# Gate tables of a PEER layer: one-hots of four tokens laid out as two contiguous blocks of two tokens

## The chip, the core and the metric

One core of a Trainium2 chip runs the whole program as one launch. The metric is the device time of that launch in microseconds. Before the change it is 3511.7 us, the median of three runs (3500.95 to 3513.11).

The engines that matter here: PE (TensorE), which runs matmuls and loads their weights (PEld); DVE (VectorE); ACT (ScalarE); POOL (GpSimd); and the queues that start transfers. Each engine runs its own instructions in a fixed order and waits on semaphores for the others.

## What is computed

One layer of a decoder over 1056 tokens: a token mixer (RWKV7 and pooling), then PEER, a layer of 16384 single-neuron experts of which each token uses 8 x 16, then an embedding gate and a norm. The change lies in PEER. Cut to that:

```python
s1 = jnp.einsum('thc,nc->thn', q[:, :, 0], sub_keys[0]);  s2 = ...(q[:, :, 1], sub_keys[1])
v1, i1 = lax.top_k(s1, 16);  v2, i2 = lax.top_k(s2, 16)
cand = v1[..., :, None] + v2[..., None, :]                # 256 candidates per head
sc, ci = lax.top_k(cand, 16)
expert = e1 * 128 + e2                                     # e1, e2: the two keys chosen
gate = softmax(sc)
act = gelu(einsum('thkd,td->thk', u_tab[expert], xb)) * gate
out = einsum('thk,thkd->td', act, v_tab[expert])
```

## The kernel before

The 1056 tokens are split. The first 672 are "dense": for them the kernel multiplies with all 16384 experts and scales the result by a gate table, which is zero for experts that a token does not use. The other 384 tokens gather the rows of their experts.

The program has three stages. First come the mixer and its projections (to about 520 us). Then, for four groups of tokens, three streams are interleaved by hand (`merge`): the recurrent chunks, the projections of PEER (`phase_c`, with matmuls at lines 661 to 663 and 747), and the selection of experts (`top` and `select`, many short DVE instructions at 762 to 850), at whose end the gate tables of dense tokens are made. Last comes the dense phase (`ublock`, `ugate`, `vblock`, line 1075), in which PE multiplies with the expert tables while GpSimd fetches rows for the other tokens. The order of the instructions on each engine is fixed when the program is built, by a scheduler that follows the order of the program and its own estimates.

A gate table is made like this. For one token, the table over the 128 x 128 experts is a product of two one-hot matrices: the 128 choices of the token lie on the partitions, `e16[:, 0]` and `e16[:, 1]` hold the two keys of each choice, `e16[:, 2]` and `e16[:, 3]` the upper and lower part of its gate in f16. The loop at 871 does four tokens at a time, 168 times in all (672 / 4). The tile `ab` (three buffers, f16) holds three blocks for four tokens, and the four tokens are innermost: [128 partitions, 3, 128 keys, 4 tokens].

- Line 875 (DVE): both one-hots in one instruction of 1024 elements, the keys `iota16` compared with `e16[:, 0:2]`, into blocks 0 and 1.
- Line 877 (DVE): block 2 = block 1 times the upper part of the gate, 512 elements.
- Line 878 (`GLO`, defined at 1043): block 1 = block 1 times the lower part, 512 elements; on GpSimd (through `PTT`, line 124), but on DVE where t is a multiple of 12, 58 times.
- Line 881 (PE): eight f16 matmuls of 128 x 128 x 128; weights are blocks 2 and 1, the moving operand is block 0. Token i is read with `[:, k, :, i]`, every fourth element.
- Line 882 (ACT): PSUM, four tokens of 128 columns, to the staging tile `st`; after 32 tokens line 884 stores it.

`iota16` is written once, by an iota on GpSimd (1040) and a cast on DVE (1041).

Of the kernel before, what the change touches and what calls it, by code (L numbers as in the profile page):

```python
# [10 lines left out]
F32 = mybir.dt.float32  # L11
F32R = mybir.dt.float32r
F16 = mybir.dt.float16
# [3 lines left out]
ALU = mybir.AluOpType  # L17
# [29 lines left out]
TC = 32  # L47
NTC = ND // TC
EB = 128
# [12 lines left out]
def body(ctx, tc, io):  # L62
    nc = tc.nc
    mm = nc.tensor.matmul
    TT, STT, TS, ACT = (nc.vector.tensor_tensor, nc.vector.scalar_tensor_tensor, nc.vector.tensor_scalar,
                        nc.scalar.activation)
# [17 lines left out]
    def v3(ap, n):  # L84
        return ap.rearrange("p (a b) -> p a b", b=n)
# [5 lines left out]
    def vec(base, i):  # L91
# [13 lines left out]
                   allow_small_or_imprecise_dtypes=True)  # L105
# [20 lines left out]
    def PS(tag):  # L126
        return pools[tag].tile([128, 512], F32, name="ps", tag=tag)
# [625 lines left out]
    def top(tk, pos, m):  # L753
        V12 = tk.tile([128, HEADS, 2, TOPK], F32, name="V12", bufs=1)
        I12 = tk.tile([128, HEADS, 2, TOPK], U32, name="I12", bufs=1)
        for i in range(16):
            if i % 4 == 0:
                sq = tk.tile([128, 4, 128], F32, name="scq", bufs=2)
                nc.sync.dma_start(sq[:m], sc_d[TIDX[pos], :m, i:i + 4, :])
            s_ = sq[:m, i % 4, :]  # L760
            v8, i8 = V12[:m, i // 2, i % 2, :], I12[:m, i // 2, i % 2, :]
            nc.vector.max(v8[:, 0:8], s_)
            nc.vector.max_index(i8[:, 0:8], v8[:, 0:8], s_)
            s2 = tk.tile([128, 128], F32, name="s2", bufs=2)
            nc.vector.match_replace(s2[:m], v8[:, 0:8], s_, -BIG)
            nc.vector.max(v8[:, 8:16], s2[:m])
            nc.vector.max_index(i8[:, 8:16], v8[:, 8:16], s2[:m])
            yield
        yield from select(tk, pos, m, V12, I12)


    def select(tk, col, m, V12, I12):
# [6 lines left out]
        for src, dst, add in ((V12, cand, TT), (F12, code, PTT)):  # L779
            off = 0  # L780
            for a, b, w in SEG:
                k = b - a
# [77 lines left out]
        ps = PS("b3")  # L860
# [3 lines left out]
        e16 = gp.tile([128, 4, 128], F16, name="e16")  # L864
# [4 lines left out]
        for t1 in range(0, m, TC):  # L869
            st = gp.tile([128, EB, TC], F32, name="gst", bufs=2)  # L870
            for t2 in range(0, TC, 4):
                ps = PS("b3")
                t = t1 + t2
                ab = gp.tile([128, 3, EB, 4], F16, name="ab", bufs=3)
                TT(ab[:, 0:2], iota16[:, None, :, :].to_broadcast([128, 2, EB, 4]),  # L875
                   e16[:, 0:2, None, t:t + 4].to_broadcast([128, 2, EB, 4]), op=ALU.is_equal)
                TT(ab[:, 2], ab[:, 1], e16[:, 2, None, t:t + 4].to_broadcast([128, EB, 4]), op=ALU.mult)  # L877
                GLO(t)(ab[:, 1], ab[:, 1], e16[:, 3, None, t:t + 4].to_broadcast([128, EB, 4]), op=ALU.mult)
                for i in range(4):
                    for k in (2, 1):  # L880
                        mm(ps[:, i * 128:(i + 1) * 128], ab[:, k, :, i], ab[:, 0, :, i], start=k == 2, stop=k == 1)  # L881
                ACT(st[:, :, t2:t2 + 4].rearrange("p e t -> p t e"), v3(ps, 128), AF.Copy, scale=1.0 / GS)  # L882
                yield
            nc.sync.dma_start(g_d[:, :, (col + t1 - GA) // TC].rearrange("g p e t -> p g e t"), st.rearrange("p (g e) t -> p g e t", e=GQ))
# [150 lines left out]
    tk = phases.enter_context(tc.tile_pool(name="tk", bufs=1))  # L1035
    gstack = ExitStack()
    gp = gstack.enter_context(tc.tile_pool(name="gp", bufs=1))
    iota16 = gp.tile([128, EB, 4], F16, name="iota16")
    it = gp.tile([128, EB, TC], F32, name="gst", bufs=2)[:, :, 0:4]
    nc.gpsimd.iota(it, pattern=[[1, EB], [0, 4]], base=0, channel_multiplier=0, allow_small_or_imprecise_dtypes=True)  # L1040
    nc.vector.tensor_copy(iota16, it)

    def GLO(t):
        return PTT if t % 12 else TT
# [125 lines left out]
    for col in range(0, GT, 128):  # L1170
# [31 lines left out]
        for half in range(2):  # L1202
            ps = dpt.tile([128, 512], F32, name="pt")
# [151 lines left out]
def program(arrays, extra=()):  # L1355
    nc = bacc.Bacc("TRN2", target_bir_lowering=False, num_devices=1)
    io = {k: nc.dram_tensor(k, v.shape, mybir.dt.from_np(v.dtype), kind="ExternalInput").ap()
          for k, v in arrays.items()}
    for k, s in list(OUTS.items()) + list(extra):
        io[k] = nc.dram_tensor(k, s, F32, kind="ExternalOutput").ap()  # L1360
    with tile.TileContext(nc, schedule_with_timeline_sim=True) as tc, ExitStack() as ctx:
        body(ctx, tc, io)
    return nc
# [15 lines left out]
```

## Time and profile before

| what | value |
|---|---|
| median of three runs | 3511.7 us |
| the profiled execution's own time | 3494.25 us |
| its span, first to last instruction | 3492.4 us |
| PE busy | 3262.7 us (93%) |
| DVE busy | 2675.0 us (77%) |
| POOL busy | 1769.3 us (51%) |
| ACT busy | 1179.8 us (34%) |
| first one-hot (line 875) to last start of an eviction (line 882) | 771.8 to 1370.6 us |

How to read it: all of it comes from one profiled execution, traced by the hardware. A busy time is the time during which an engine has at least one instruction running. Matmuls and DVE instructions are pipelined, so the shown time of one can overlap that of the next; what one costs in a row of its kind is the distance from start to start. [...] A share over the whole span is a mean over stages that have different limits.

### The profile page before, as it was taken

Reading aid. Unit: us, or ns where it says so; the run is one execution under the profiler, and the core shown is the slowest. Engines: PE = TensorE matmul, PEld = TensorE weight load, DVE = VectorE, ACT = ScalarE, POOL = GpSimd, SP = SyncE. Lnnn points to the kernel's source line nnn. Section 1 sums busy time; section 2 is a strip of 40 time slices with the busy share of each in tenths; the row PEclk is TensorE's granted clock in tenths of the full one; section 3 lists DMA queues with packets and bytes.
Section 4 is the critical chain, followed back from the end, with each engine's and each line's share of the span. In section 5 each row is a group of like instructions: output and inputs, shape, how many; then the busy total and the mean of one; then the engine's idle time right before and its main releaser. Section 6 shows DMA issues by size and latency. Waiting matters only on the chain.

```text
span 3492.4 us, 57600 instructions
## 1 busy us (share of the span) xinstructions
PE 3262.7 (93%) x21831; PEld 3150.6 (90%) x21831; DVE 2675.0 (77%) x5366; ACT 1179.8 (34%) x1776; POOL 1769.3 (51%) x1433
## 2 busy tenths in 40 slices
PE   8997998999999899999999999999999999999997
PEld 7876998989989788999999999999999999999997
DVE  6767333279999799978788778878888787788866
ACT  6452424345556455322122122122122212222243
POOL 5434234145465454156656555555555565555635
PEclk9998999999999899999999999999999999999999
DMA  5667645767767867479888888889898898898834
GB/s 177 213 197 177 185 134 148 213 174 231 210 194 212 282 199 258 131 278 318 308 315 307 306 320 311 313 318 317 314 321 315 307 312 308 301 318 313 311 123 132
DMA packets 467861, 883.61 MB, mean 253 GB/s; under 512 B 129280, under 2 KB 252416, under 8 KB 463104
## 3 DMA queue, kind: packets, MB, share of 16 engines
q1 hardware_dynamic: 356992, 477.24, 43.5%
q0 software_dynamic: 110592, 402.70, 32.6%
q8 instruction: 171, 2.80, 0.3%
q14 instruction: 106, 0.87, 0.1%
HBM read 759.22 MB, written 120.60 MB: 252 GB/s over the span
## 4 chain that ended last, share of the span: by engine, by line
DMA 26%; PE 22%; DVE 19%; issue 14%; POOL 11%; ACT 1%; SPq 0%; POOLq 0%; DVEq 0%; ACTq 0%
DMA row<-v,idx 14%; POOL row L1179 10%; DMA row<-u,idx 7%; PE pd L1075 7%; PE ps L881 2%; DVE ab L875 2%; PE ps L663 2%; PE ps L661 2%; DVE row L1187 2%; PE ps L662 2%; DVE elo L1063 1%; DVE po L1196 1%; PE ps L526 1%; DVE ab L877 1%; DMA sraw<-wq 1%
## 5 line engine op out<-in xcount | busy, mean ns | idle before, releaser
L1179 POOL DMA_INDIRECT row<-u,idx x384 | 534.9, 1393 | 387.9 <-DVE row L1187 248.4
L1179 POOL DMA_INDIRECT row<-v,idx x384 | 520.5, 1355 | 377.3 <-DVE po L1196 222.4
L1196 DVE SCALAR_TENSOR_TENSOR po<-row,act,po 128x1024 f32<-128x1024 f32 x381 | 488.8, 1283 | 152.6 <-DMA row<-v,idx 147.8
L1187 DVE SCALAR_TENSOR_TENSOR row<-row,xt 128x1024 f32<-128x1024 f32 x384 | 463.6, 1222 | 179.4 <-DMA row<-u,idx 177.8
L1075 PE MATMUL pd<-XH,elo 128*128 128x336 f32 x2176 | 524.9, 323 | 52.2 <-DVE elo L1063 49.3
L1061 ACT ACTIVATE ehi<-eraw 128x1024 fp32r<-128x1024 f32 x278 | 293.0, 1054 | 750.3 <-PE pd L1075 676.1
L1075 PE MATMUL pd<-wh,elo 128*128 128x336 f32 (+1 forms) x2112 | 509.5, 320 | 31.2 <-DVE elo L1063 30.9
L1075 PE MATMUL pd<-XH,ehi 128*128 128x336 f32 x2176 | 518.0, 319 | 4.1 <-DVE OT L1150 2.3
L1075 PE MATMUL pd<-XL,ehi 128*128 128x336 f32 x2176 | 519.5, 320 | 0.0
L1075 PE MATMUL pd<-wh,ehi 128*128 128x336 f32 (+1 forms) x2112 | 506.5, 319 | 8.7 <-DVE tg L1260 6.3
L1075 PE MATMUL pd<-wl,ehi 128*128 128x336 f32 (+1 forms) x2112 | 504.3, 318 | 0.0
L1075 PEld LDWEIGHTS pd<-XH,elo 128*128 128x128 f32 x2176 | 376.9, 191 | 64.4 <-DVE elo L1063 61.5
L1075 PEld LDWEIGHTS pd<-wh,elo 128*128 128x128 f32 x2112 | 362.1, 189 | 40.1 <-DVE elo L1063 39.4
L1075 PEld LDWEIGHTS pd<-XH,ehi 128*128 128x128 f32 x2176 | 377.7, 192 | 5.1 <-ACT wt L1081 2.5
L1075 PEld LDWEIGHTS pd<-XL,ehi 128*128 128x128 f32 x2176 | 376.7, 191 | 0.2
L1075 PEld LDWEIGHTS pd<-wh,ehi 128*128 128x128 f32 x2112 | 364.2, 189 | 10.5 <-issue 8.4
L1075 PEld LDWEIGHTS pd<-wl,ehi 128*128 128x128 f32 x2112 | 364.3, 189 | 0.0
L1063 DVE TENSOR_TENSOR elo<-eraw,ehi 128x1024 fp32r<-128x1024 f32 x257 | 317.9, 1237 | 11.7 <-ACT ehi L1061 6.3
L1140 ACT ACTIVATE wh<-wt 128x672 fp32r<-128x672 f32 x128 | 97.5, 766 | 662.1 <-DVE wt L1138 662.1
L881 PE MATMUL ps<-ab 128*128 128x128 f16 x1344 | 195.9, 295 | 25.0 <-DVE ab L877 12.0
L124 POOL TENSOR_TENSOR ab<-ab,e 128x512 f16<-128x512 f16 x110 | 128.4, 1169 | 172.2 <-DVE ab L877 130.7
L882 ACT ACTIVATE gst<-ps 128x512 f32<-128x512 f32 x168 | 179.5, 1103 | 94.4 <-PE ps L881 92.5
(499 smaller groups left out, 5962.7 us busy)
## 6 DMA issues: line engine op xcount, KB each, us to landing
eraw<-uT SPq DMA_DIRECT2D x128, 512.0 KB, 5.4
eraw<-vP SPq DMA_DIRECT2D x128, 512.0 KB, 5.7
g_d<-gst SPq DMA_DIRECT2D x21, 2048.0 KB, 8.4
gq<-g_d SPq DMA_DIRECT2D x32, 1344.0 KB, 9.4
whi<-wc_d SPq DMA_DIRECT2D x148, 256.0 KB, 4.4
wlo<-wc_d SPq DMA_DIRECT2D x148, 256.0 KB, 4.7
wc_d<-shi SPq DMA_DIRECT2D x40, 256.0 KB, 2.6
wc_d<-slo SPq DMA_DIRECT2D x40, 256.0 KB, 3.1
```

The source lines that it names most:

```text
L124: nc.gpsimd.tensor_tensor(out, a, b, op=op)
L661: mm(ps[:, :n], whi[:, kk, :], xhi[:, k, :n], start=k == 0, stop=False)
L662: mm(ps[:, :n], whi[:, kk, :], xlo[:, k, :n], start=False, stop=False)
L881: mm(ps[:, i * 128:(i + 1) * 128], ab[:, k, :, i], ab[:, 0, :, i], start=k == 2, stop=k == 1)
L882: ACT(st[:, :, t2:t2 + 4].rearrange("p e t -> p t e"), v3(ps, 128), AF.Copy, scale=1.0 / GS)
L1061: ACT(hi, raw, AF.Copy)
L1063: sub(lo, raw, hi.bitcast(F32), op=ALU.subtract)
L1075: mm(ps[:, a, :n], w_[:, k, :], x_[:, s:s + n], start=first, stop=last)
L1140: ACT(wh, wt_, AF.Copy)
L1179: nc.gpsimd.indirect_dma_start(out=r[:m], out_offset=None, in_=io[tab], in_offset=bass.IndirectOffsetOnAxis(ap=idx[:m, hh, k:k + 1], axis=0))
L1187: STT(r[:m], r[:m], 1.0, xt[:m], op0=ALU.mult, op1=ALU.mult, accum_out=pre[:m, k:k + 1])
L1196: STT(po[:m], r[:m], act[:m, k:k + 1], po[:m], op0=ALU.mult, op1=ALU.add)
```

## The change

`ab` becomes [128 partitions, 3, 2 pairs, 128 keys, 2 tokens]: each of the three blocks has two contiguous halves, one for each pair of tokens, and within a half the two tokens alternate. `iota16` has two copies of each key instead of four. Line 875 becomes two instructions, one for each one-hot, of 512 elements each. The operand taken from `e16` is read as pairs: two pairs, each repeated for 128 keys, two elements in a row instead of four. The matmul of token i reads every second element of its half. The number of matmuls, their order and their results' place stay.

```diff
-                ab = gp.tile([128, 3, EB, 4], F16, name="ab", bufs=3)
-                TT(ab[:, 0:2], iota16[:, None, :, :].to_broadcast([128, 2, EB, 4]),
-                   e16[:, 0:2, None, t:t + 4].to_broadcast([128, 2, EB, 4]), op=ALU.is_equal)
-                TT(ab[:, 2], ab[:, 1], e16[:, 2, None, t:t + 4].to_broadcast([128, EB, 4]), op=ALU.mult)
-                GLO(t)(ab[:, 1], ab[:, 1], e16[:, 3, None, t:t + 4].to_broadcast([128, EB, 4]), op=ALU.mult)
+                ab = gp.tile([128, 3, 2, EB, 2], F16, name="ab", bufs=3)
+
+                def pairs(j):
+                    return e16[:, j, t:t + 4].rearrange("p (a b) -> p a b", b=2)[:, :, None, :].to_broadcast([128, 2, EB, 2])
+
+                io16 = iota16[:, None, :, :].to_broadcast([128, 2, EB, 2])
+                for j in range(2):
+                    TT(ab[:, j], io16, pairs(j), op=ALU.is_equal)
+                TT(ab[:, 2], ab[:, 1], pairs(2), op=ALU.mult)
+                GLO(t)(ab[:, 1], ab[:, 1], pairs(3), op=ALU.mult)
                 for i in range(4):
                     for k in (2, 1):
-                        mm(ps[:, i * 128:(i + 1) * 128], ab[:, k, :, i], ab[:, 0, :, i], start=k == 2, stop=k == 1)
+                        mm(ps[:, i * 128:(i + 1) * 128], ab[:, k, i // 2, :, i % 2], ab[:, 0, i // 2, :, i % 2],
+                           start=k == 2, stop=k == 1)
...
-    iota16 = gp.tile([128, EB, 4], F16, name="iota16")
-    it = gp.tile([128, EB, TC], F32, name="gst", bufs=2)[:, :, 0:4]
-    nc.gpsimd.iota(it, pattern=[[1, EB], [0, 4]], base=0, channel_multiplier=0, allow_small_or_imprecise_dtypes=True)
+    iota16 = gp.tile([128, EB, 2], F16, name="iota16")
+    it = gp.tile([128, EB, TC], F32, name="gst", bufs=2)[:, :, 0:2]
+    nc.gpsimd.iota(it, pattern=[[1, EB], [0, 2]], base=0, channel_multiplier=0, allow_small_or_imprecise_dtypes=True)
```

## Rows read from the trace of the kernel before

**Rows 1.** The page: busy time with share and instructions; busy tenths in 40 slices

```profile
PE 3262.7 (93%) x21831; PEld 3150.6 (90%) x21831; DVE 2675.0 (77%) x5366; ACT 1179.8 (34%) x1776; POOL 1769.3 (51%) x1433
...
PE   8997998999999899999999999999999999999997
...
DVE  6767333279999799978788778878888787788866
```

**Rows 2.** Stretches: length, busy PE, PEld, DVE, ACT, POOL (instructions), clock, DMA, GB/s

```profile
771.00:1372.00 601.00, 555.24 (x4386) 527.36 (x4385) 563.88 (x2134) 332.48 (x509) 315.14 (x311) 0.95 0.75 222
...
960.00:1160.00 200.00, 187.63 (x1558) 178.84 (x1556) 196.65 (x780) 117.24 (x194) 109.15 (x112) 0.99 0.70 205
1160.00:1240.00 80.00, 67.45 (x471) 61.06 (x471) 60.48 (x171) 38.84 (x51) 35.47 (x35) 0.81 0.88 286
```

**Rows 3.** Waits of DVE, 771 to 1372 us: total, times, longest

```profile
DVE ab L875 <- PE ps L881: 21.9, 18, 9.0
```

**Rows 4.** Groups, 771 to 1372 us: busy, mean ns | idle before, releasers

```profile
L881 PE MATMUL ps<-ab 128*128 128x128 f16 x1344 | 195.9, 295 | 25.0 <-DVE ab L877 12.0 <-DVE ab L878 4.4 <-ACT gst L882 3.6
...
L875 DVE TENSOR_TENSOR ab<-iota,e 128x1024 f16<-128x1024 f16 x168 | 147.2, 885 | 23.8 <-PE ps L881 21.9 <-POOL ab L124 1.2
...
L877 DVE TENSOR_TENSOR ab<-ab,e 128x512 f16<-128x512 f16 x168 | 91.0, 551 | 0.3
...
L507 DVE TENSOR_TENSOR lts<-ps,ident 128x512 f32<-128x512 f32 x6 | 4.1, 689 | 0.2
```

**Rows 5.** Single lines: durations ns min/median/max, first and last start

```profile
L875 DVE TENSOR_TENSOR ab<-iota,e x168: 659/682/2708, 771.8 to 1363.4; 128x1024 f16<-128x1024 f16 x168
...
L877 DVE TENSOR_TENSOR ab<-ab,e x168: 366/412/2326, 779.6 to 1365.5; 128x512 f16<-128x512 f16 x168
...
L124 POOL TENSOR_TENSOR ab<-ab,e x110: 1029/1044/2404, 781.7 to 1366.1; 128x512 f16<-128x512 f16 x110
L124 POOL TENSOR_TENSOR ltm<-lts,nmt x81: 736/1291/2260, 330.8 to 1119.5; 128x512 f32<-128x512 f32 x80, 64x256 f32<-64x256 f32 x1
```

**Rows 6.** Chain of waits by line: 771 to 1372 us, then 1300 to 1372 us

```profile
by line: PE ps L881 11.7%; DVE ab L875 11.6%; DVE ab L877 6.8%; PE ps L661 4.1%; PE ps L663 4.1%; PE ps L662 3.9%; DVE oh L847 3.3%; DMA wlo<-wc_d 3.3%; DVE h L718 2.9%; issue 2.7%; PE ps L526 2.1%; DVE I L763 2.0%; DVE s L765 2.0%; DVE ab 
...
by line: PE ps L881 25.7%; DMA wlo<-wc_d 17.3%; PE ps L663 10.9%; PE ps L661 10.6%; PE ps L662 10.0%; PE ps L747 5.8%; DMA xt_d<-xt 5.1%; DVE ab L875 3.8%; issue 2.9%; ACT gst L882 1.5%; DVE ab L878 1.2%; SPq L650 1.1%; POOL oh L124 1.0%; D
```

**Rows 7.** Timeline: start us, length us, engine, line; near 1094, then 1101 us

```profile
1092.13 0.68 DVE L875 TENSOR_TENSOR ab<-iota,e 128x1024 f16<-128x1024 f16 x1
1092.73 0.47 DVE L766 MAX8 V<-s 128x8 f32<-128x128 f32 x2
...
1094.91 0.41 DVE L877 TENSOR_TENSOR ab<-ab,e 128x512 f16<-128x512 f16 x1
1095.25 0.42 DVE L878 TENSOR_TENSOR ab<-ab,e 128x512 f16<-128x512 f16 x1
...
1101.38 1.73 POOL L124 TENSOR_TENSOR ltm<-lts,nmt 128x512 f32<-128x512 f32 x1
...
1101.89 1.51 DVE L877 TENSOR_TENSOR ab<-ab,e 128x512 f16<-128x512 f16 x1
```

**Rows 8.** Timeline of PE, runs of one line merged; four places

```profile
1115.75 1.10 PE L881 MATMUL ps<-ab 128*128 128x128 f16 x8
...
1118.17 0.38 PE L519 MATMUL ps<-id 128*128 128x512 f16 x1
1118.39 0.83 PE L521 MATMUL ps<-Y,ltm 128*128 128x128 f32 x6
...
2006.46 0.47 PE L1075 MATMUL pd<-XL,ehi 128*128 128x336 f32 x2
2006.76 0.47 PE L1075 MATMUL pd<-XH,elo 128*128 128x336 f32 x2
...
437.08 1.26 PE L553 MATMUL ps<-ssm,apb 128*64 128x64 f32 x18
```

**Rows 9.** The cast of the key table: duration ns, first and last start

```profile
L1041 DVE CAST iota<-gst x1: 1493/1493/1493, 535.5 to 535.5; 128x512 f16<-128x512 f32 x1
```

## The prediction

> **What bounds the kernel now.** I read the page first, for engines and slices. TensorE is busy 93% of the span; from about 1480 us its slices read 9 to the end, so the dense expert phase behind the tables is its own [rows 1]. The tables are made earlier, and there VectorE's slices also read 9 [rows 1]. So the question is which of the two sets the pace of that stretch. The table of stretches answers in part: in the 601 us from the first one-hot to about the last table matmul, DVE is busy 563.9 us and PE 555.2 us; from 960 to 1160 us DVE is busy 196.65 of 200; only 1160 to 1240 us is loose on both (60.5 and 67.5 of 80) [rows 2]. Everything behind this stretch waits for its end: the gates are needed by the dense phase, and PE has no gap later in which a delay would vanish. Then the waits: in the same stretch the one-hot instruction is held 18 times by the table matmuls, 21.9 us in all [rows 3], and the table matmuls in turn are held for 25.0 us, mostly by DVE's products at 877 and 878 [rows 4]. The two engines hold each other, and DVE has less room: it is idle 601 - 563.9 = 37 us, 22 of them in these waits.
>
> PE's busy figure flatters it, since the time shown for one matmul overlaps the next (an f16 table matmul shows 295 ns [rows 4], but eight run in 1.10 us [rows 8]). I worked PE's need out from start-to-start times: a table matmul costs (1.10 - 0.295)/7 = 0.115 us, so 1344 of them [rows 4] are 155 us of PE's stretch. The table loop runs 168 times, for four tokens each.
>
> The chain of waits through this stretch is shared: 11.7% of it is table matmuls (70 us), 11.6% the one-hot instruction (70 us), 6.8% the product at 877 (41 us); near the end of the stretch, 1300 to 1372 us, table matmuls alone are 25.7% of the chain (18 us) [rows 6].
>
> **The change, part by part.**
>
> *One DVE instruction more per loop.* The 1024-element one-hot becomes two of 512 elements. Their medians: 682 ns for 1024, 412 ns for 512 with the same kind of operands [rows 5]. But DVE starts the next instruction before the shown end of the last: a 1024 is followed after 0.60 us (1092.13 to 1092.73), a 512 after 0.34 us (1094.91 to 1095.25) [rows 7]. 512 more elements cost 682 - 412 = 270 ns, so 0.34 - 0.27 = 0.07 us of a 512 is the instruction itself, and the second instruction adds that much: 168 x 0.07 = 12 us of DVE (the shown durations would give 2 x 412 - 682 = 142 ns, 24 us: the upper end).
>
> *A second start per loop that GpSimd can catch.* The mean of the one-hot is 885 ns against a median of 682, of 877's product 551 against 412 [rows 4, 5]. The excess comes where a GpSimd elementwise instruction is running: 877 at 1101.89 took 1.51 us while a GpSimd product ran from 1101.38 to 1103.11 [rows 7]. An added instruction of the same size and kind may pay 551 - 412 = 139 ns: 168 x 0.139 = 23 us as upper end. [...] I take a third, 8 us.
>
> *Rows of two instead of four elements in the operands.* Packed 16-bit speed shows in the 412 ns for 512; the 4-byte form of 512 elements takes 689 ns [rows 4]. No f16 operand in rows of two is in this trace, so a 512 costs between 412 and 689. [...] GpSimd's product, two loops in three, takes 1044 ns now and its 4-byte sibling 1291 [rows 5]: bounds 0 and 110 x 0.25 = 27 us of GpSimd, which is half idle in the stretch (315 of 601 us [rows 2]). I take 0.
>
> *The table matmuls read every second element instead of every fourth.* This is where the gain would be. A table matmul of 128 columns reads one f16 in 8 bytes, over 1024 bytes, and costs 115 ns. The only contiguous f16 matmul, 512 columns over the same 1024 bytes, starts at 1118.17 and the next at 1118.39: 0.22 us, or 0.42 ns a column [rows 8]; at that rate 128 columns are 54 ns. So the table matmul does not run at the column rate. The 4-byte dense matmul reads 336 columns, 1344 bytes, in (2006.76 - 2006.46)/2 = 0.15 us [rows 8]: 0.114 ns a byte spanned, and 1024 x 0.114 = 117 ns, the table matmul's cost. By that, what limits it is the span that it reads. With the step halved the span is 512 bytes: 58 ns. Pairs of a weight load and a matmul can follow each other about that fast: 18 of 64 columns in 1.26 us, 0.07 us each or less [rows 8]. Bounds: 58 ns (all of it) and 115 ns (none of it); I take 62. Then PE's stretch gets 1344 x 53 = 71 us lighter, and a group of eight ends 0.4 us sooner.
>
> [...]
>
> *What is moved or set up once.* The order of the matmuls, the PSUM layout, the eviction and the stores stay as they are; no queue gets a new wait. The iota and its cast halve, once, before the stretch: nothing, since the cast starts at 535.5 us [rows 9] and the first one-hot that reads it at 771.8 [rows 5].
>
> **What the path gets.** DVE: 12 + 8 = +20 us, nearly all on the path, as DVE is 94% busy in the stretch. PE: 71 us lighter, but it counts only where DVE or the end of the stretch waits for it. The 18 waits of the one-hot for table matmuls [rows 3] each end one or two groups sooner, 18 x 0.4 to 0.8 = 7 to 14 us; I take 11. In the loose part, 1160 to 1240 us, and at the end of the stretch the chain runs over PE, but there DVE is again nearly full from 1240 on, so only some 5 us come back. Sum: 20 - 11 - 5 = +4 us. The rest of PE's gain turns into PE waiting for DVE, which shows as more idle time before the table's weight loads. Bounds of the sum: DVE +12 to 24 + 23 = +47, PE's return 0 to 37 (all of DVE's idle time).
>
> The profiled execution took 3494.25 us (span 3492.4), 17 us less than the median of the runs, 3511.7; the sum is made on it and carried to the median: 3511.7 + 4 = 3516 us.
>
> **Rivals.**
> B, faster: PE sets the pace in the stretches where the chain runs over it, and DVE's order slides together. Then the 70 us of table matmuls on the chain shrink by (115 - 62)/115 = 46%, 32 us, against 8 us added to the one-hot pieces of the chain (70/0.885 = 79 instructions x 0.1): -24 us, 3488. For it: 25.7% of the chain at the end of the stretch [rows 6]. Against it: DVE's 196.65 of 200 [rows 2]; a chain changes over to the next engine as soon as one shortens.
> C, slower: GpSimd catches the added starts as often as 877's. It decides once the extra 139 ns are paid in more than about two loops of three: 12 + 23, with 5 us returned, +30 us, 3542. For it: the present one-hot already pays 885 - 682 = 203 ns on the mean. Against it: GpSimd's instructions are no more than now.
> D: the step was not what held the table matmuls (issue or the weight load was), and they stay near 115 ns. Nothing comes back: +20, 3532. Against it: the price by bytes, and pairs at 0.07 us.
> E: rows of two lose the packed rate. From start to start a 512 is then 0.689 - 0.07 = 0.62 us: +0.64 for the two one-hots, +0.28 for 877's product and for the 58 of 878's that DVE makes (t a multiple of 12): 168 x 0.92 + 58 x 0.28 = +171 us, some 3680. For it: nothing but that no row shows rows of two. Against it: the packed rate with rows of four.
>
> **How the numbers follow.** A change of 0.5% (17.5 us) is about what a measurement of this kernel tells from none. The forecast, within 0.5%, gets 0.50 (own range 3496 to 3529, from the bounds of the return and of the caught starts); B 0.24; C 0.16; D 0.06, E 0.04. Faster is B: 0.24. Same is the forecast: 0.50. Slower is C, D and E: 0.26. The range runs from 3484, leaving out the deeper half of B, to 3548, which takes in C and D and leaves out E.
>
> **What would show it.** Right: eight table matmuls in about 0.65 us instead of 1.10; two 512 one-hots at medians near 412 ns and 0.34 us apart; GpSimd's product near 1044 ns; DVE's busy time in the table stretch up by 10 to 25 us, and more PE idle put down to lines 875 to 878; the stretch from first one-hot to last table eviction within 15 us of now, about 600 us. Wrong: a stretch shorter by over 20 us with DVE idle falling (B); means far over the medians for both one-hots (C); groups still at 1.1 us (D); 512s near 690 ns (E). What I can't weigh from this trace: with PE waiting more, its clock may be granted at the lower level for longer, as in the loose part now (mean 0.81 [rows 2]), and the instruction order around the loop may come out differently.

## The result, and the profile after

The changed kernel takes 3534.0 us (median of 8 runs, 3526.7 to 3561.0), the kernel before, beside it on the same chip, 3510.3 us: a ratio of 1.0085, with a 95% interval of 1.0056 to 1.0114. By the medians that is 24 us slower, by the ratio, which everything below goes by, 30 us. The forecast was +4: the time lies inside the range given, 18 us over the forecast of 3516, and past the half per cent that tells a difference from none.

The page of the changed kernel: its span, busy time by engine, and two rows of the 40 slices, as in [rows 1]. The traced execution took 3550.8 us, 17 more than the median of its runs, where the traced one of before took 16 less; so the two spans are not compared.

```profile
span 3548.9 us, 57780 instructions
...
PE 3237.7 (91%) x21831; PEld 3112.1 (88%) x21831; DVE 2701.7 (76%) x5534; ACT 1172.8 (33%) x1776; POOL 1758.0 (50%) x1433
...
PE   8996998988888788999999999999999999999997
...
DVE  6767333279999898988787778777878787787866
```

VectorE has 168 instructions more (5534 against 5366), as it must, and 27 us more work; TensorE has 25 us less. In the slices the table part differs (the ninth to the sixteenth): TensorE's 9s there have become 8s, and VectorE's row hardly changes.

The table of stretches (length, busy PE, PEld, DVE, ACT, POOL with instructions, clock, DMA share, GB/s), first over the same times as [rows 2], then over the changed kernel's own stretch from its first one-hot to its last table eviction:

```profile
771.00:1372.00 601.00, 501.16 (x4245) 465.70 (x4243) 571.18 (x2256) 313.92 (x497) 295.85 (x300) 0.92 0.73 214
960.00:1160.00 200.00, 164.60 (x1481) 152.88 (x1479) 191.14 (x773) 111.25 (x191) 107.14 (x111) 0.98 0.71 201
1160.00:1240.00 80.00, 62.45 (x472) 55.91 (x473) 67.46 (x211) 34.85 (x51) 28.05 (x29) 0.74 0.78 248
```

```profile
779.80:1408.10 628.30, 520.02 (x4418) 482.59 (x4418) 597.89 (x2336) 327.25 (x513) 313.08 (x314) 0.92 0.72 213
```

The stretch lasts 628.3 us where it lasted 600.0 (771.8 to 1371.8), and VectorE is still busy 95% of it (597.9). TensorE's share falls from 92% to 83%. In the dense middle, 960 to 1160 us, VectorE shows 191 of 200 us where it showed 197, and TensorE 165 instead of 188.

The parts of the change by themselves came out as predicted, by the medians. Durations of single lines (ns min/median/max, first and last start), for the one-hots (881), the product (882) and GpSimd's product by the lower part of the gate, to be read against [rows 5]:

```profile
L881 DVE TENSOR_TENSOR ab<-iota,e x336: 393/414/2621, 779.8 to 1402.8; 128x512 f16<-128x512 f16 x168
...
L882 DVE TENSOR_TENSOR ab<-ab,e x168: 361/411/4561, 786.7 to 1404.0; 128x512 f16<-128x512 f16 x168
...
L124 POOL TENSOR_TENSOR ab<-ab,e x110: 1030/1046/2331, 790.0 to 1404.5; 128x512 f16<-128x512 f16 x110
```

And one group of eight table matmuls in TensorE's timeline, against the 1.10 us of [rows 8]:

```profile
1120.18 0.62 PE L886 MATMUL ps<-ab 128*128 128x128 f16 x8 [0.65 <-ACT gst L888]
```

The matmuls come 57 ns apart ((0.62 - 0.22)/7; the median of one is shown with 218 ns), half of before. TensorE waits for VectorE with the time it saved. Groups from 771 to 1372 us (busy, mean ns, then idle time before them and its releasers), against [rows 4]; they hold 1248 of the 1344 matmuls, since the rest now come later:

```profile
L881 DVE TENSOR_TENSOR ab<-iota,e 128x512 f16<-128x512 f16 x316 | 171.5, 585 | 19.6 <-PE ps L886 17.1 <-ACT e L866 2.2
...
L886 PE MATMUL ps<-ab 128*128 128x128 f16 x1248 | 119.7, 232 | 65.6 <-DVE ab L882 29.0 <-ACT gst L888 14.6 <-DVE ab L883 13.6
```

The idle time before the table matmuls rises from 25.0 to 65.6 us. The mean of the one-hots, 585 ns, lies far over their median of 414; I come back to that. VectorE's own wait, the line to set against [rows 3] (us in all, times, longest):

```profile
DVE ab L881 <- PE ps L886: 17.1, 10, 4.0
```

**Where the end comes from.** The chain of waits that ended last, from the page of the changed kernel (shares of the span by engine, then by line), shows no row of the table part:

```profile
DMA 21%; issue 11%; PE 11%; POOL 7%; DVE 7%; ACT 0%; POOLq 0%; DVEq 0%; ACTq 0%
DMA row<-v,idx 14%; PE pd L1081 11%; POOL row L1185 7%; DMA row<-u,idx 6%; DVE po L1202 2%; DVE row L1193 2%; DVE elo L1069 1%; DVE OT L1156 1%; DVE wt L1144 0%; DVE OT L1282 0%; DVE wl L1148 0%; DVE tg L1268 0%; DVE wl L1234 0%; DVE GH L1282 0%; POOLq L1185 0%
```

That is not proof that the tables are off the path: the shares add up to 57% of the span, which is the stretch from the first row gather to the end, and there this chain breaks off. The chain of before does not break off, and the table part is in it (`ps` at 881 and `ab` at 875, some 70 us each):

```profile
DMA 26%; PE 22%; DVE 19%; issue 14%; POOL 11%; ACT 1%; SPq 0%; POOLq 0%; DVEq 0%; ACTq 0%
DMA row<-v,idx 14%; POOL row L1179 10%; DMA row<-u,idx 7%; PE pd L1075 7%; PE ps L881 2%; DVE ab L875 2%; PE ps L663 2%; PE ps L661 2%; DVE row L1187 2%; PE ps L662 2%; DVE elo L1063 1%; DVE po L1196 1%; PE ps L526 1%; DVE ab L877 1%; DMA sraw<-wq 1%
```

Between the tables and the first gather it runs over the last projections (747) and the load of the scores that they make (`scq`), then over the last two selects:

```profile
1397.99 1.80 PE ps L747 x16
...
1406.90 3.25 DMA scq<-sc_d
```

Both chains run through the 768 row gathers that GpSimd starts for the tokens which get no tables. Their first start, from the timeline of GpSimd, in before and in after:

```profile
1499.82 1.50 POOL L1179 DMA_INDIRECT row<-u,idx  x1 [1.70 <-DVE gl L850]
```

```profile
1537.19 1.17 POOL L1185 DMA_INDIRECT row<-u,idx  x1 [2.50 <-DVE wt L1144]
```

From that start to the end of the span there are 1992.6 us in before (3492.4 - 1499.8) and 2011.7 in after; over the eleven kernels tabulated below it is 1984 to 2012, with no clear relation to how slow the kernel is. So, as far as single traces show it, what the change does to the time, it does ahead of the first gather, which starts 13 to 18 us behind the last select's row numbers (`idx`, line 852): 1486.4 us in before, 1519.9 in after. The last two selects are VectorE's and come behind the tables in its queue. That distance, counted from each trace's own first one-hot, is the measure in what follows: 728.0 us to the first gather before, 757.4 after, 29.4 more. (The traces begin their one-hots between 771.3 and 779.8 us, also where the order up to there is the same; so I count from there.)

### The profile page after: what moved, and what is told of

Read it like the earlier page. It is cut to its first block, busy times and chain, and to the rows that moved or that the text cites. A ratio compares the mean times of both kernels' runs of the same rounds, so it can differ in the third digit from the quotient of the medians.

```text
span 3548.9 us, 57780 instructions
## 1 busy us (share of the span) xinstructions
PE 3237.7 (91%) x21831; PEld 3112.1 (88%) x21831; DVE 2701.7 (76%) x5534; ACT 1172.8 (33%) x1776; POOL 1758.0 (50%) x1433
## 4 chain that ended last, share of the span: by engine, by line
DMA 21%; issue 11%; PE 11%; POOL 7%; DVE 7%; ACT 0%; POOLq 0%; DVEq 0%; ACTq 0%
DMA row<-v,idx 14%; PE pd L1081 11%; POOL row L1185 7%; DMA row<-u,idx 6%; DVE po L1202 2%; DVE row L1193 2%; DVE elo L1069 1%; DVE OT L1156 1%; DVE wt L1144 0%; DVE OT L1282 0%; DVE wl L1148 0%; DVE tg L1268 0%; DVE wl L1234 0%; DVE GH L1282 0%; POOLq L1185 0%
## 5 line engine op out<-in xcount | busy, mean ns | idle before, releaser
L1185 POOL DMA_INDIRECT row<-v,idx x384 | 532.1, 1386 | 400.2 <-DVE po L1202 224.2
L1185 POOL DMA_INDIRECT row<-u,idx x384 | 518.9, 1351 | 383.9 <-DVE row L1193 245.8
L1081 PEld LDWEIGHTS pd<-wh,ehi 128*128 128x128 f32 x2112 | 367.7, 191 | 17.6 <-issue 15.1
L661 PE MATMUL ps<-hi,whi 128*128 128x256 f32 (+1 forms) x592 | 183.4, 311 | 22.4 <-DMA whi<-wc_d 12.0
```

The source lines that it names most:

```text
L661: mm(ps[:, :n], whi[:, kk, :], xhi[:, k, :n], start=k == 0, stop=False)
L1081: mm(ps[:, a, :n], w_[:, k, :], x_[:, s:s + n], start=first, stop=last)
L1185: nc.gpsimd.indirect_dma_start(out=r[:m], out_offset=None, in_=io[tab], in_offset=bass.IndirectOffsetOnAxis(ap=idx[:m, hh, k:k + 1], axis=0))
```

## The experiments

The framework sets each engine's instruction order anew from the program, and the added instruction changes far more than its place: TensorE's list of after differs from that of before in some 1680 rows. So there were three theories at first. Theory 1: the added VectorE instruction is the price. Theory 2: the other order is. Theory 3: TensorE, idle more often, is granted a lower clock, and other matmuls pay (the clock granted in the trace of before reads 1.00 or 0.50, and 0.50 all the time from 1200 to 1220 us). All ratios are to the kernel before, run beside, each with its 95% interval.

**One one-hot, step of two.** The gates `e16` are laid out as [32, 4, 4] so that one instruction of 1024 can make both one-hots in the new layout. The order stays that of before, row for row on TensorE.

```
-        e16 = gp.tile([128, 4, 128], F16, name="e16")
+        e16 = gp.tile([128, 32, 4, 4], F16, name="e16")
...
+                TT(ab[:, 0:2].rearrange("p j a e b -> p (j a) e b"), iota16[:, None, :, :].to_broadcast([128, 4, EB, 2]),
+                   pairs(0, 2), op=ALU.is_equal)
```

> The changed layout (steps of two, two blocks of pairs), but both one-hots made by one instruction of 1024 elements, as before the change; only the key tile e16 is laid out otherwise for it. PE's order is that of the kernel before, instruction for instruction. Theory 1 (VectorE is the limit, and its added instruction is the price): the price is gone and some of PE's gain comes back, 16 us by the terms of the prediction (11 + 5): ratio to before 0.9955, between 0.990 and 0.999. Theory 2 (the planner's other order of instructions is the price): the order is that of before, so a ratio at or a little under 1, between 0.993 and 1.000. Theory 3 (a faster TensorE idles more, is granted its lower clock for longer, and all other matmuls pay for it): slower than before, 1.003 to 1.010, with the granted clock in the table stretch at about 0.92 as after the change, not 0.95 as before.

Measured: 0.9999 (0.9978 to 1.0019). Halving the step of 1344 matmuls gives nothing, and costs nothing, that the interval (-8 to +7 us) tells from zero. Groups of this kernel from 771 to 1372 us:

```profile
L880 DVE TENSOR_TENSOR ab<-iota,e 128x1024 f16<-128x1024 f16 x168 | 146.5, 881 | 16.9 <-PE ps L886 16.5
...
L886 PE MATMUL ps<-ab 128*128 128x128 f16 x1344 | 125.5, 228 | 58.5 <-DVE ab L882 28.6 <-DVE ab L883 9.9 <-ACT gst L888 9.3
```

The matmuls' shown time falls from 195.9 to 125.5 us, and their idle time rises from 25.0 to 58.5: half of the gain is back as waiting right there. VectorE's waits on them fall by 5.4 us (21.9 to 16.5). Theory 3 loses its case: TensorE has the saving, its clock in the stretch is 0.94 against 0.95, and nothing is slower.

**Split alone.** The layout and step of before, two one-hots of 512. Its order is that of after, row for row on TensorE.

```
-                TT(ab[:, 0:2], iota16[:, None, :, :].to_broadcast([128, 2, EB, 4]),
-                   e16[:, 0:2, None, t:t + 4].to_broadcast([128, 2, EB, 4]), op=ALU.is_equal)
+                for j in range(2):
+                    TT(ab[:, j], iota16, e16[:, j, None, t:t + 4].to_broadcast([128, EB, 4]), op=ALU.is_equal)
```

> The layout before the change (steps of four), with the one-hots split into two instructions of 512 elements. The order of the instructions on every engine is that of the changed kernel, as far as the instructions are the same. Theory 1 (the added VectorE instruction): +20 us against before with nothing returned, 3532; slower than the changed kernel or equal to it: ratio to before 1.005 to 1.014. Theory 2 (the order): the same ratio, since it has both; this run doesn't tell 1 from 2. Theory 3 (lower clock because of faster matmuls): the table matmuls are at 115 ns again, so close to before, 0.997 to 1.003.

Measured: 1.0096 (1.0069 to 1.0124). The split alone costs what the whole change costs, with matmuls as in before and a clock of 0.95 from 771 to 1372 us, where Theory 3 forecast no change. But it brings both the instruction and the order.

**Two other orders.** The kernel before with one number of its interleaving by hand altered: a length declared to `merge`, `t_len` of the selection stream or `b_len` of the recurrent chunks. The instructions are the same on all engines.

```
-                n += 24 + m // 4
+                n += 23 + m // 4
```

```
-        return (cb - ca) * 26
+        return (cb - ca) * 26 + 1
```

> The kernel before, with one number of the hand-made interleaving changed: the length that is declared for the selection stream, 23 in place of 24 steps per tile. The instructions are the same, each with its operands and its cost; their order differs from before as much as that of the changed kernel does (some 1950 lines of TensorE's list against 1680). Theory 1 (the added instruction) and theory 3 (clock): no change, 0.997 to 1.003. Theory 2 (order): any time within about 1% of before, in either direction, and at least one of the two reordered kernels outside 0.997 to 1.003.

> The kernel before, with another number of the hand-made interleaving changed: the length that is declared for the recurrent chunks' stream, longer by one. Same instructions, another order (some 1010 lines of TensorE's list differ). Theory 1 and theory 3: no change, 0.997 to 1.003. Theory 2 (order): any time within about 1% of before, in either direction.

Measured: 1.0069 (1.0044 to 1.0094) and 1.0097 (1.0074 to 1.0120). An order alone, with not one instruction more, costs as much as the change. So Theory 2 can carry it; whether it does, these runs can't say, because the order of after is another one.

**Order and instruction taken apart.** Four runs edit the instruction list once the order is settled, so that nothing else moves. In the first, each one-hot of before is cut into two neighbours (the first half keeps the wait, the second the signal); the second does so to the kernel with the step of two; the third joins 161 of the 168 pairs of the split kernel into one; the fourth cuts into four. The cut of the first, where `part` makes an instruction like `i` on a part of its operands:

```
+    N = 2
+    w = 1024 // N
+    return [part(nc=None, i=i, name=i.name if k == N - 1 else f"I-{900000 + 4 * n + k}", first=k == 0, last=k == N - 1,
+                 out=([[1536, 128], [1, w]], k * w),
+                 ins=[([[512, 128], [1, w]], k * w % 512),
+                      ([[512, 128], [0, w // 4], [1, 4]], k * w // 512 * 128)]) for k in range(N)]
```

> The kernel before, its instruction order on every engine left untouched: only, once the order is settled, each of the 168 one-hot instructions of 1024 elements is cut into two neighbours of 512. Same matmuls, same step of four. Theory 1 (the added VectorE instruction is the price): as slow as the split with its own order, 3520 to 3532 us, +12 to +24 us on the kernel before. Theory 2 (the other order of instructions is the price): the kernel before within 8 us, 3490 to 3506.

> The whole change (step of two, two one-hots of 512, the layout in which one instruction could make both) in the instruction order of the kernel before: each one-hot of the run with one instruction is cut in two after the order is settled. Theory 1: 3520 to 3534 us, the time of the changed kernel. Theory 2: 3495 to 3510 us, no slower than the kernel before by more than 10 us.

> The reverse: the split kernel with the order of the changed kernel (step of four), but after the order is settled 161 of its 168 pairs of one-hots are joined into one instruction of 1024 (the seven whose halves are not neighbours stay apart). Theory 1: back to 3498 to 3510 us, since the added instruction is gone. Theory 2: still slow, 3522 to 3532, since the order is that of the changed kernel.

> A larger dose at the order of the kernel before: each one-hot of 1024 elements is cut into four neighbours of 256, three added VectorE instructions in each of 168 loops. VectorE's work grows by about 3 x 0.07 x 168 = 35 us. Theory 1 (VectorE sets the pace): +30 to +45 us, 3528 to 3543. Theory 2 with slack on VectorE: below half of it, up to +17 us, 3498 to 3515.

Measured, with the distances from the first one-hot in each trace and VectorE's one wait for the load of the dense phase's gates (`wt<-wt,gq`); the next runs' rows stand in it too:

| kernel | order | one-hots per loop | step | to last `idx`, us | to first gather, us | wait for gates, us | ratio (95%) |
|---|---|---|---|---|---|---|---|
| before | before | 1 | 4 | 714.6 | 728.0 | 4.9 | 1 |
| one one-hot | before | 1 | 2 | 710.4 | 723.8 | 6.5 | 0.9999 (0.9978-1.0019) |
| cut in two | before | 2 | 4 | 726.0 | 739.4 | 3.9 | 1.0042 (1.0022-1.0061) |
| whole change | before | 2 | 2 | 729.3 | 742.7 | 5.3 | 1.0020 (1.0003-1.0037) |
| cut in four | before | 4 | 4 | 752.3 | 765.7 | 5.3 | 1.0127 (1.0100-1.0153) |
| cleared | before | none | 4 | 687.5 | 700.9 | 5.3 | 0.9911 (0.9889-0.9934) |
| joined | after | 1 | 4 | 729.8 | 747.4 | 12.7 | 1.0040 (1.0016-1.0064) |
| split alone | after | 2 | 4 | 734.8 | 752.4 | 12.6 | 1.0096 (1.0069-1.0124) |
| after | after | 2 | 2 | 740.1 | 757.4 | 11.8 | 1.0085 (1.0056-1.0114) |
| `t_len` 23 | a third | 1 | 4 | 733.7 | 749.2 | 14.5 | 1.0069 (1.0044-1.0094) |
| `b_len` + 1 | a fourth | 1 | 4 | 741.5 | 755.1 | 15.9 | 1.0097 (1.0074-1.0120) |

Neither theory holds alone. The instruction by itself costs 0.42%, 15 us (Theory 1 said 12 to 24; Theory 2 at most 8). The order by itself costs 0.40%, 14 us (Theory 1 said none, Theory 2 14 to 24). The whole change in the order of before, +7 us, came as Theory 2 said, and the cut in four, +45 us, as Theory 1 said. The sum of the two single prices, 0.82%, is the split's 0.96% and the change's 0.85% within the intervals. The step of two is worth 0.01% with one one-hot, 0.22% with two in the order of before (1.0042 to 1.0020) and 0.11% in that of after: nothing that stands clear of the intervals. The larger dose fits a price per instruction: three more per loop put the first gather 37.7 us later, 0.075 us for each of 504; one more puts it 11.4 later, 0.068 us for each of 168. In other pairs of the table one more instruction measures otherwise: 7 us of time and 18.9 of distance with the step of two, 20 us and 5.0 in the order of after. Likewise the order costs 14 us with one one-hot, but 19 with two, and 23 between the two kernels with the whole change (1.0085 against 1.0020). The intervals allow one price for each, and do not show it.

VectorE's work grows by more than the added instructions, since some of its instructions are stretched beside GpSimd: in before, of the 336 one-hots and products at 875 and 877, 101 show over 15% more than their median, and all 101 run beside a GpSimd tensor instruction. Summed over the loop's one-hots and products on VectorE, what they show over the median of their form is 68.6 us in before, 77.3 cut in two, 78.0 cut in four, 81.4 joined, 96.6 in the split alone and 93.9 in after. Group of the cut one-hots, 776.3 to 1502.3 us, and two of them from start to start with what follows (0.67 us, where one of 1024 took 0.60 [rows 7]):

```profile
L875 DVE TENSOR_TENSOR ab<-iota,e 128x512 f16<-128x512 f16 x336 | 176.9, 570 | 19.5 <-PE ps L881 19.1
...
1099.43 0.75 DVE L875 TENSOR_TENSOR ab<-iota,e 128x512 f16<-128x512 f16 x2
1100.10 0.41 DVE L878 TENSOR_TENSOR ab<-ab,e 128x512 f16<-128x512 f16 x1
```

All the cut one-hots of the first of these four runs and its first gather, then the third's: its wait for the gates (us in all, times, longest), on which the order's part shows, and its first gather:

```profile
L875 DVE TENSOR_TENSOR ab<-iota,e x336: 390/414/2626, 776.3 to 1381.6; 128x512 f16<-128x512 f16 x168
```

```profile
1515.71 1.50 POOL L1179 DMA_INDIRECT row<-u,idx  x1 [1.70 <-DVE gl L850]
```

```profile
DVE wt L1138 <- DMA gq<-g_d: 12.7, 1, 12.7
```

```profile
1522.10 1.15 POOL L1179 DMA_INDIRECT row<-u,idx  x1 [2.76 <-DVE wt L1138]
```

That wait tells the orders apart: 3.9 to 6.5 us in all six kernels with the order of before, 11.8 to 15.9 in the five with another. VectorE stands there, just behind the tables, with the last two selects behind it in its queue. It is 7.8 (12.7 - 4.9) of the 15.2 us that `joined` loses up to the last `idx`, less 1.0 that other waits give back; 8.4 more are VectorE's busy time, 678.2 against 669.8 us up to there (the 168 products at 877 alone show 104.3 us instead of 92.6, each counted in full). By place it looks otherwise: the table stretch of `joined` is 17.9 us longer than that of before (617.9 against 600.0), and the part from there to the last `idx` is 2.7 us shorter (111.9 against 114.6), since the order does some 12 us of VectorE's later work ahead of the last table. And the first gather follows `idx` after 17.6 us instead of 13.4; its releaser above is now a gate multiplication (`wt`, 1138) where it was the last select's `gl`. The next runs were to tell how much of the order's price each of these carries; that is not settled.

**The gate multiplications moved to GpSimd, and the one-hots cleared.** Two further theories. P: VectorE's queue up to the last select sets the first gather and with it the end. Q: TensorE's dense phase sets the end by itself. The first edit takes the first ten gate multiplications and their subtractions off VectorE, in before, in after, and in the kernel with one one-hot and the step of two; the second replaces each one-hot of before by a clearing of the same elements, in the order of before, and so computes no tables.

```
-        TT(w3, w3, gqs[0][:, :, b % GQ, :], op=ALU.mult)
+        sub = PTT if b < 10 else TT
+        sub(w3, w3, gqs[0][:, :, b % GQ, :], op=ALU.mult)
...
-        TT(wl, wt_, wh.bitcast(F32), op=ALU.subtract)
+        sub(wl, wt_, wh.bitcast(F32), op=ALU.subtract)
```

```
+    return [mybir.InstMemset(mode="Const", constant=0, name=i.name, engine=i.engine, debug=i.debug, ins=[], outs=list(i.outs),
+                             descendants=i.descendants, sync_info=i.sync_info, bass_priority=i.bass_priority,
+                             bass_scheduled_tick=i.bass_scheduled_tick, bass_scheduled_proc=i.bass_scheduled_proc,
+                             bass_scheduled_scope=i.bass_scheduled_scope)]
```

> The kernel before, with the first ten gate multiplications of the dense phase and their ten subtractions on GpSimd instead of VectorE (table part unchanged). In the trace of before VectorE does them between the last table and the last select, about 10 x 0.85 + 10 x 0.85 = 17 us, and stands 4.9 us for the load of their gates. Theory P (VectorE's queue up to the last select sets the first gather, and that the end): first gather and time earlier by 12 to 22 us, 3486 to 3496 where the kernel before has 3508. Rival Q (TensorE's dense phase sets the end by itself): no gain, 3500 to 3515.

> The same edit on the changed kernel, whose VectorE stands 11.8 us for that load instead of 4.9. Theory P: 17 us of work and the 11.8 us of waiting leave VectorE's queue ahead of the last select: 20 to 29 us earlier than the changed kernel, 3506 to 3516 us, and the distance to the kernel before with the same edit shrinks by some 7 us against the distance of the unedited two. Rival Q: 3530 to 3540, as the changed kernel.

> The same edit on the kernel with a step of two and one one-hot of 1024 (order of the kernel before). Theory P: 12 to 22 us under the kernel before, 3486 to 3496, the candidate to beat both. Rival Q: 3500 to 3515.

> The kernel before in its own order, where each of the 168 one-hots of 1024 elements is replaced by a clearing of the same 1024 elements on VectorE (the tables are not computed). How long a clearing takes no trace shows; if it is d us shorter from start to start than the 0.60 us of the one-hot, VectorE has 168 x d less. Theory P: the time falls by most of 168 x d until the table matmuls' pace takes over (for d = 0.3: 25 to 50 us, 3458 to 3483). Rival Q: within 10 us of the kernel before.

Measured, the moved gates: 1.0050 (1.0033 to 1.0068) on before, 1.0068 (1.0048 to 1.0089) on after, 1.0032 (1.0016 to 1.0048) with one one-hot. Both forecasts missed: no gain of 12 to 22 us, and on before not even no change, but a loss of 17. What P got wrong is that the edit would bring the first gather forward. Its distance went from 728.0 to 737.0 us on before, from 757.4 to 756.7 on after and from 723.8 to 740.4 with one one-hot, and the time moved with it: +17, -6 and +12 us. Waits of VectorE from 1372 to 1503 us in the edited kernel before:

```profile
DVE V L762 <- DMA scq<-sc_d: 18.0, 3, 9.1
```

The same wait there was 0.7 us before. VectorE, freed of the gates, waits for scores: the last projection group, which makes them, ends about 8 us later (last eviction at line 742 at 1413.2, where it was 1397.4, of which 7.6 us are this trace's later start). In between TensorE waits for the low halves of the dense weights, `elo`, GpSimd's among them, which now stand among the gate multiplications in GpSimd's queue. TensorE's waits and GpSimd's groups from 1372 to 1503 us in this kernel:

```profile
PE pd L1075 <- DVE elo L1063: 5.9, 2, 4.1
PE ps L663 <- POOL elo L124: 4.4, 1, 4.4
```

```profile
L124 POOL TENSOR_TENSOR wl<-wt,wh 128x672 fp32r<-128x672 f32 x9 | 15.5, 1755 | 7.7 <-ACT wh L1141 7.7
L124 POOL TENSOR_TENSOR wt<-wt,gq 128x672 f32<-128x672 f32 x9 | 14.4, 1618 | 3.6 <-DMA gq<-g_d 3.6
```

By these means GpSimd needs 1.76 and 1.62 us, where VectorE's medians for the same two instructions in before are 0.85. A wait was moved, not removed. On after the edit changes little (1.0085 to 1.0068). The two edited kernels lie 0.18% apart, where the unedited ones lie 0.85%, but mostly because before became slower, by waits that the edit brought. What part the gate multiplications' place has in the order's price is therefore not shown.

The clearing (single line, then one from start to start with what follows, then VectorE's wait on the table matmuls, then the first gather):

```profile
L875 DVE MEMSET ab<- x168: 485/485/485, 776.1 to 1336.4; 128x512 uint32 x168
...
1081.68 0.48 DVE L875 MEMSET ab<- 128x512 uint32 x1
1082.08 0.36 DVE L877 TENSOR_TENSOR ab<-ab,e 128x512 f16<-128x512 f16 x1
```

```profile
DVE ab L875 <- PE ps L881: 42.1, 41, 8.5
```

```profile
1477.03 1.50 POOL L1179 DMA_INDIRECT row<-u,idx  x1 [1.70 <-DVE gl L850]
```

From start to start a clearing takes 0.40 us where a one-hot that is not stretched took 0.60, so d is 0.2 and 168 x d is 34 us. The first gather comes 27.1 us sooner (700.9 against 728.0) and the time falls by 0.89%, 31 us: Theory P by its own count. But the clearings are not stretched either, where the one-hots showed 203 ns over their median on the mean [rows 4, 5], and VectorE's busy time up to the last `idx` falls by 65.9 us (669.8 to 603.9). Less than half of that comes through. VectorE's idle time up to there rises from 44.8 to 83.6 us, and 20.2 of that are waits for the table matmuls (42.1 us in 41 waits instead of 21.9 in 18 [rows 3]): TensorE begins to set the pace. So most of the work added to VectorE in the table loop shows up in the first gather (11.4 of 16.3 us for one instruction, 37.7 of 40.8 for three), and of the work taken away less than half.

Over all these runs the time follows the first gather: against the kernel before, the two differences never lie more than 10 us apart, over gathers from 27 us sooner to 38 us later. No version that computes the tables beats the kernel before.

## Why the prediction was right, and where it failed

**The number: in part luck.** The range of 3484 to 3548 holds the 3534 because it took in rivals C and D. The forecast's own range, 3496 to 3529, does not hold it, and slower, which came, had a chance of 0.26. More than half of the loss, 14 to 23 us, comes from a cause that the sum did not have, the order.

**VectorE sets the pace of the table stretch: right.** Three doses at one order (one instruction more, three more, a cheaper one) move the first gather by +11.4, +37.7 and -27.1 us, and the time by +15, +45 and -31. TensorE's halved step moves neither by more than the intervals allow. That holds for added work; with 65.9 us of VectorE's work gone, TensorE begins to set the pace.

**One instruction more per loop, +12 us: right at the order of before.** 11.4 us of distance, 15 us of time; 0.07 us each from start-to-start times was the right reading, not the 0.142 of the shown durations.

**Starts that GpSimd can catch, +8 us: right in size at the order of before.** What the instructions of the loop show over their medians grows from 68.6 to 77.3 us, by 8.7: the one-hots' part by 18, while the products behind them give 10 back. With the 12 that makes 20; VectorE's busy time up to the last `idx` grew by 16.3. Cut in four it is 9.4, so it is not paid for each start, as rival C had it. In the change's own order it is 25.3, the sign that I named for C came (a mean of 589 ns against a median of 414), and C's +30 is what the ratio gives. But the order without the added instruction already shows 12.8 of the 25.3 (`joined`). C is out at the order of before, and half right for the changed kernel. That the forecast took a third of its upper end of 23 was a guess: no run shows that share.

**Rows of two at 412 ns; GpSimd's product: right.** With rows of two the one-hot's 512 and the product took 414 and 411 ns, with rows of four the product took 412; GpSimd's product took 1046 against 1044. The sum takes the lower end of the bounds 412 and 689, and no row of before showed that end for rows of two: it was a guess, which the changed kernel's trace bears out. Rival E is out.

**Step of two, 58 instead of 115 ns: right.** 57 ns by the group above, at a step of 4 bytes, where 8 bytes took 115. Rival D's cause is out; its sum, +20 with nothing returned, 3532, lies nearest to the time, since TensorE's gain did not come through. The price by bytes was less sure than it looked: the f32 matmul that it was read from takes 0.15 us for 336 columns, 0.45 ns a column, so it may have gone at the rate by columns. At a step of 4 bytes both prices give nearly the same, 58 and 54 ns.

**TensorE's return, -11 and -5 us: the term that was mis-sized.** I let each of the 18 waits of the one-hot end one or two groups sooner. With one one-hot and the order of before, 21.9 us became 16.5, a third of the 16 us claimed, the distance to the first gather fell by 4.2 us and the time by nothing (0.9999); with two one-hots the ratio fell by 0.22% (8 us), while the distance rose by 3.3 us. Between 0 and 8 us, and not told from 0. Rival B is out for the same reason: a chain that runs over TensorE for a quarter of its length at the end of the stretch [rows 6] is no promise that TensorE's gain comes through.

**The sum at an unchanged order:** +12 + 8 - 16 = +4 was forecast, and the whole change in the order of before measures 1.0020 (1.0003 to 1.0037), +7 us. VectorE's 20 show as 17.6 us of busy time up to the last `idx`, and its first gather comes 14.7 us later. So the time agrees with the sum better than the path does, where little of the 16 is seen.

**The order: the step that was missing.** The prediction named it among what it could not weigh and gave it no term. The order costs 14 us with one one-hot (0.40%, 0.16 to 0.64) and 23 between the two kernels with the whole change, and with it the forecast of +4 becomes +18 to +27, where 24 (medians) and 30 (ratio) were measured. The change adds a node to a schedule that is built anew, so a term for the order, of either sign, belonged in the range. Two orders tried at random cost 0.69% and 0.97%: the order of before is the best of the four, which no row of its trace says.

**"Everything behind this stretch waits for its end": imprecise.** The end of the tables is on the path, but does not set the end alone. The chain goes back to the first gather, that to the last select, and that through VectorE's queue, behind the tables, behind the first gate multiplications and behind the scores of the last projection group. For the added instruction it made no odds, as the delay passes on whole. For the order of after it made little: the table stretch is 17.9 us longer and the first gather 19.4 us later (`joined`). For another order it made all the odds: with `b_len` + 1 the table stretch is 3.3 us shorter than before (596.7), and the first gather still comes 27 us later.

**Of what I said would show it:** the group of eight (0.62 us), the 414 ns, GpSimd's 1046 ns and more idle before the table matmuls came; VectorE's busy time rose by 35 us over its stretch (562.9 to 597.9) instead of 10 to 25, and the stretch grew by 28 instead of at most 15. Some 11 of the 35 are later work that the new order does within the stretch: up to the last `idx` it is 24.0 (669.8 to 693.7).

**Left open:** how the 14 us of the order divide into the wait for the gates, the longer instructions and the later first gather. Holding the rest of the order and moving VectorE's gate multiplications alone behind the last select was not tried. Nor does any run separate the first gather from the start of TensorE's dense phase, which comes behind the same tables and projections.

## What to carry to other kernels

Where a planner orders the instructions, test an edit in two ways: as the planner takes it, and with the old order held, the instruction list edited afterwards; without the second, an order's price is taken for the edit's. Weigh an edit by the engine whose queue leads to the start of the last long chain (here VectorE up to the first gather), and check that with one dose more and one less on that engine: a saving on the other engine was worth nothing here that could be told from zero, however exactly it was foretold, and a saving on the bounding one paid less than half, as it then waited for the other. A busy engine's wait is not removed by giving its work to an idle one whose queue feeds the same chain (here 17 us slower on the kernel before).

## What the hardware showed

- The f16 matmul of 128 columns comes 115 ns after the one before with a step of 8 bytes and 57 with 4, and the shown weight loads, whose columns have the same step, fell from a mean of 119 to 104 ns (771 to 1372 us). Between these two steps the time went with the bytes spanned. At 4 bytes it is 0.45 ns a column, about that of the contiguous f16 and the f32 matmul (0.42 and 0.45 [rows 8]), so bytes alone don't set it. Both operands have the step, and no run tells which of them set the 115 ns.
- A clearing of 1024 f16 on VectorE (as 512 of uint32) took 485 ns in all 168 places, though GpSimd ran beside it as before; the two-operand one-hots in its place went from 659 to 2708 ns [rows 5]. Of the 93 clearings that stand alone in the timeline 55 ran beside a GpSimd tensor instruction, and none was stretched: these instructions, which read no operand, took the same time beside GpSimd as without it.
- Each one-hot instruction added, with the elements the same, put the first gather 0.068 us later (two of 512 for one of 1024) and 0.075 us (four of 256, median 279 ns).
